# Giving each step's streamed weights their own start inside the ring buffers

## The chip, the cores and the metric

The kernel runs on one core of a Trainium2 chip. The metric is the device time of one execution in microseconds; the times given are medians of several runs. A profile shows one execution, with its own time.

## The reference

One layer of a hybrid model for a sequence of 256 tokens and a width of 1024, all in float32:

```python
h = _rmsnorm(x, norm_w) * (1 + scale) + shift          # shift, scale, gate = split(c @ w_ada + b_ada)
(qa, ka, va, za, qm, km, vm, zm, om, ig, fg, ga, gm) = jnp.split(h @ w_in, SPLIT_IDX, axis=-1)
qa, ka = _rmsnorm(heads(qa), q_norm_w), _rmsnorm(heads(ka), k_norm_w)
ya = (merge(_moba_attention(qa, ka, heads(va), rel_bias)) * jax.nn.silu(za)) @ w_att_proj
qm, km = jnp.split(jax.nn.silu(_causal_dwconv(jnp.concatenate([qm, km], -1), conv_w, conv_b)), 2, -1)
hm = jax.nn.sigmoid(om) * _mlstm_chunkwise(qm, km * ML_HEAD_DIM ** -0.5, vm, ig + b_igate, fg + b_fgate)
hm = _rmsnorm(hm, ml_norm_w)
ym = (merge(hm) * jax.nn.silu(zm)) @ w_ml_proj
y = jax.nn.sigmoid(ga) * ya + jax.nn.sigmoid(gm) * ym
return x + gate * (y @ w_out)
```

With 256 tokens the attention has one block, so it is plain causal attention with a bias. Most of the work is thirteen projections of 256 x 1024 by 1024 x 1024, whose weights are read once from DRAM.

## The kernel before

A first phase computes `h` and, row by row of `w_in`, the projections `qa` and most of `ka`. It leaves `h` transposed in SBUF as two parts, `hTh` and `hTl`: the value as it stands in the matmul format float32r, and the remainder. Every weight is split in the same way into `wh` (high) and `wl` (low), and each product is the sum of three matmuls: high by high, high by low, low by high.

The second phase, which the change touches, is a list of chunks, each half a projection (512 columns) and four steps long; a step covers two blocks of 128 rows of a weight. Three kinds differ in which operand TensorE holds and which it streams:

- `tok` (`ka`, `va`, `out`): a 128 x 128 block of the activations is held (stationary), and the weights are streamed (moving), up to 512 columns at once. Lines 1160 to 1162; the last chunk of `out` is written apart, lines 1184 to 1186, as one group of 512 columns and two groups of 256.
- `str` (`zm`, `vm`, `om`): a whole projection by Strassen's seven products in 14 steps of six matmuls. The weights, or sums of weight blocks, are streamed too (lines 1149 to 1151), against `hTh`, `hTl` or the sums `Sh`, `Sl` of their blocks.
- `ws` (`za`, `qm`, `km`, `att`, `ga`, `gm`, `ml`): the weights are held and the activations streamed, 256 columns at once (lines 1170, 1174, 1175). 24 matmuls a step.

`split(g)` prepares step `g`: ScalarE casts the loaded weights into `wh` (line 461, or 459 for `ml`), and VectorE, or GpSimd in ten steps, subtracts it from the weights into `wl` (line 467, or 465). It runs four steps ahead of the matmuls, in two rings of five buffers, `wh` and `wl`. A ring buffer holds `RING = 1152` floats a partition (4608 bytes), of which a step uses 1024, as two rows of 512. The order of all work is that of the code, per engine; hooks (`at`, `between`, `ahead`) place the attention, the gates and the mLSTM between the steps. In each ring buffer a `ws` step begins at float `WS_AT = 80`, and every other step at 0.

The two rings, `hTh` and `hTl` lie at fixed places: each ring buffer begins at a multiple of 512 bytes in its partition, `hTh` and `hTl` 256 bytes past one, and their blocks of 128 columns follow 512 bytes apart.

Of the kernel before, what the change touches and what calls it, by code (L numbers as in the profile page):

```python
# [10 lines left out]
F32R = mybir.dt.float32r  # L11
# [13 lines left out]
RING, WS_AT = 1152, 80  # L25
# [39 lines left out]
def tile_hybrid(ctx: ExitStack, tc: tile.TileContext, x, c, params, params2, rel_t, w_row, ada_mod, ada_gate,  # L65
# [89 lines left out]
    def modulate(k, parts="ij"):  # L155
        kc = slice(k, k + 1)
        if "i" in parts:
            nc.scalar.activation(hTh[:, k], xnT[:, k], AF.Identity, scale=Ab[:, kc], bias=Bb[:, kc])
        if "j" not in parts:
            return  # L160
        hf[k] = ph.tile([128, S], F32, name="hf", bufs=2)
        nc.scalar.activation(hf[k], xnT[:, k], AF.Identity, scale=Ab[:, kc], bias=Bb[:, kc])
# [96 lines left out]
    def some(*what):  # L259
        return lambda k: [mm_row(k, ch, (i,)) for ch, i in what]  # L260
# [19 lines left out]
    for step in P1_STEPS:  # L280
        op, k = step[0], int(step[1])
        if op == "L":
            next_loads(k)
        else:
# [5 lines left out]
                 a=modulation_scale, b=modulation_shift, i=lambda k: modulate(k, "i"), j=lambda k: modulate(k, "j"),  # L290
                 P=lambda k: mm_row(k, 0), Q=lambda k: mm_row(k, 1, (0, 1)), q=lambda k: mm_row(k, 1, (2,)),
                 N=lambda k: mm_row(k, 2), M=lambda k: mm_row(k, 3),
                 n=some((2, 0), (2, 1), (3, 0), (3, 1)), m=some((2, 2), (3, 2)),
# [31 lines left out]
    C, step0, owner = {}, [], []  # L325
# [86 lines left out]
    hl = ctx.enter_context(tc.tile_pool(name="hl", bufs=1, reuse_waits="tile"))  # L412
# [19 lines left out]
    HB = 5  # L432
    pool_lo = set()
    pool_lo.update((step0[C["ml", 0]] + 2, step0[C["ml", 0]] + 3))
    for nm, hf in (("qm", 0), ("qm", 1), ("km", 0), ("km", 1)):
        s = (start("km") if (nm, hf) == ("qm", 1) else done(nm, hf)) + 4
        pool_lo.update((s, s + 1))

    def split(g, between=()):
        ch = chunks[owner[g]]  # L440
        if ch["kind"] == "str":
            j = g - step0[owner[g]]
            w = form(ch["name"], j // 2)[:, 2 * (j % 2):2 * (j % 2) + 2]
        else:
            li, ks, cs = raw_of[g]
            w = rawt[li][:, ks, cs]
        n = ch["n"]
        at0 = WS_AT if ch["kind"] == "ws" else 0
        h = hl.tile([128, RING], F32R, name="wh", bufs=HB)[:, at0:at0 + 1024].rearrange("p (k n) -> p k n", k=2)[:, :, 0:n]
        l = hl.tile([128, RING], F32R, name="wl", bufs=HB)[:, at0:at0 + 1024].rearrange("p (k n) -> p k n", k=2)[:, :, 0:n]  # L450
        e = nc.gpsimd if g in pool_lo else nc.vector
        kp = 2 * (g - step0[owner[g]])
        cols = [(kk, prm2[:, P_ML + kp + kk:P_ML + kp + kk + 1]) for kk in range(2)] if ch["name"] == "ml" else []
        if cols and g in pool_lo:
            for kk, wcol in cols:
                nc.scalar.activation(w[:, kk], w[:, kk], AF.Copy, scale=wcol)
            cols = []
        for kk, wcol in cols:
            nc.scalar.activation(h[:, kk], w[:, kk], AF.Copy, scale=wcol)
        if not cols:  # L460
            nc.scalar.copy(h, w)  # L461
        for fn, a in between:
            fn(*a)
        for kk, wcol in cols:
            nc.vector.scalar_tensor_tensor(l[:, kk], w[:, kk], wcol, h[:, kk].bitcast(F32), op0=OP.mult, op1=OP.subtract)
        if not cols:
            e.tensor_tensor(l, w, h.bitcast(F32), op=OP.subtract)  # L467
        whl[g] = (h, l)
# [18 lines left out]
    def form(name, p):  # L487
        if p in (1, 6):
            return T["t1" if p == 1 else "t4", name]
        return block(name, *((0, 0), None, (0, 0), (1, 0), (0, 1), (1, 1))[p])  # L490
# [48 lines left out]
    def left(p, k):  # L539
        i = (None, 0, 1, None, 2, 3, None)[p]  # L540
        if i is not None:
            return T["Sh"][:, i, k], T["Sl"][:, i, k]
        k, t = {0: (k, 0), 3: (4 + k, 0), 6: (4 + k, 1)}[p]
        return hTh[:, k, t * 128:(t + 1) * 128], hTl[:, k, t * 128:(t + 1) * 128]
# [433 lines left out]
    def ev_out(pt, c0, n, t):  # L978
# [7 lines left out]
              zm=ev_zm, vm=ev_vm, om=ev_om, ga=ev_ga, gm=ev_gm, ml=ev_ml)  # L986
# [111 lines left out]
    for g in range(A):  # L1098
        split(g)
        for fn, a in early.get(g, []):  # L1100
            fn(*a)
        consumed.update(cons.get(g, []))
    pump()
    for g in range(NG):
        ci = owner[g]
        kp = g - step0[ci]
        ch = chunks[ci]
# [5 lines left out]
        if g + A < NG:  # L1113
            split(g + A, hooks_between.get(g, []))
            consumed.update(cons.get(g + A, []))
# [24 lines left out]
        wh, wl = whl[g]  # L1140
        if ci == NCH - 1:
            continue
        if ch["kind"] == "str":
            p = kp // 2
            o = mmt[ci][(0, 2, 0, 1, 0, 2, 0)[p]]
            for kk in range(2):
                k = 2 * (kp % 2) + kk
                a, b = left(p, k)
# [4 lines left out]
        for kk in range(2):  # L1153
            k = 2 * kp + kk
            first, last = k == 0, k == KT - 1
            if ch["kind"] == "tok":
                for t in range(2):
                    a, b = sh_[:, k, t * 128:(t + 1) * 128], sl_[:, k, t * 128:(t + 1) * 128]
# [19 lines left out]
    for t, c0, n in ((0, 0, 512), (1, 0, 256), (1, 256, 256)):  # L1178
        pt = ps.tile([128, n], F32, name="mm", bufs=2)
        for k in range(KT):  # L1180
            wh, wl = whl[step0[ci] + k // 2]
            wh, wl = wh[:, k % 2, c0:c0 + n], wl[:, k % 2, c0:c0 + n]
            a, b = T["yh"][:, k, t * 128:(t + 1) * 128], T["yl"][:, k, t * 128:(t + 1) * 128]
# [51 lines left out]
```

## Time and profile before

| | |
|---|---|
| median of 3 runs | 348.6 us (348.18 to 348.78) |
| the profiled execution | 348.25 us, span 346.5 us |
| TensorE matmuls | 340.8 us busy (98% of the span), 2314 |
| TensorE weight loads | 311.9 us, beside the matmuls |
| VectorE | 293.1 us (85%) |
| ScalarE | 240.4 us (69%) |
| GpSimd | 87.8 us (25%) |
| DMA | 83.72 MB, mean 242 GB/s |

In the rows PE is TensorE, PEld its weight loads, ACT ScalarE, DVE VectorE, POOL GpSimd. A row of the timeline gives the start in us, the duration in us, the engine, the line, the operation, output and inputs, and the shape; a matmul's inputs are the tile that it streams, or the other, in the program's order of names, and `128x512` is the streamed columns. A row of a group ends with the count, the busy time in us and the mean duration in ns. A row of waits gives who waited for whom, the sum in us, the number of times, and the longest. Durations of matmuls have modelled ends: they overlap the next matmul, and the distance between two starts tells the rate.

On TensorE the stages follow one another so: the first phase to 52 us; `ka` 52.1 to 57.9; `va` 58.0 to 87, with attention scores between its steps; `za` and `qm` to 141.6; `zm` to 160.9; `km` and `att` to 209.8; `vm` to 228.9; `ga` to 250.8; `om` to 269.8; `gm` to 298.4, with the last of the mLSTM between its steps; `ml` to 320.2; `out` to the end.

### The profile page before, as it was taken

To read this page: it belongs to the slowest core of one execution; us is meant where nothing else is said; L and a number is where in the kernel's file an instruction comes from. 1 tells how busy PE (TensorE), PEld (TensorE's weight loads), DVE (VectorE), ACT (ScalarE), POOL (GpSimd) and SP (SyncE) were. 2 spreads that over 40 slices of the span, in tenths; PEclk is the share of its full clock that TensorE was granted. 3 is DMA by queue.
4 is the path that set the end of the run, shared out by engine and by line. 5 is a ranking of instruction groups with operands and counts; after the bars stand their busy time and mean duration, and the time that the engine had idled before them with its cause. 6 is when DMAs were issued, how large, how long until landed. Compare 5 with 4: busy or idle time off the path is not lost.

```text
span 346.5 us, 6040 instructions
## 1 busy us (share of the span) xinstructions
PE 340.8 (98%) x2314; PEld 311.9 (90%) x2314; DVE 293.1 (85%) x423; ACT 240.4 (69%) x372; POOL 87.8 (25%) x90
## 2 busy tenths in 40 slices
PE   8999999999999999999999999999999999999995
PEld 5887889888999999888999998899988999999885
DVE  4899994897988887999796899998988988988852
ACT  3776787989977756699688657875497768745500
POOL 4950003765200715002353273001000023400000
PEclk9999999999999999999999999999999999999999
DMA  8999999996468399188750973929969379073011
GB/s 297 417 420 422 417 387 341 235 246 274 137 231 305 58 338 296 38 304 363 268 220 2 357 195 67 387 90 350 280 188 419 113 272 384 3 270 155 0 62 61
DMA packets 29534, 83.72 MB, mean 242 GB/s; under 512 B 2109, under 2 KB 5185, under 8 KB 28994
## 3 DMA queue, kind: packets, MB, share of 16 engines
q1 hardware_dynamic: 26944, 78.08, 61.5%
q0 software_dynamic: 2112, 4.19, 7.0%
q10 hardware_dynamic: 450, 1.07, 1.0%
q8 instruction: 18, 0.29, 0.3%
q14 instruction: 10, 0.08, 0.1%
HBM read 81.89 MB, written 1.45 MB: 241 GB/s over the span
## 4 chain that ended last, share of the span: by engine, by line
PE 82%; DMA 8%; POOL 4%; DVE 2%; ACT 2%; issue 1%; SPq 0%; DVEq 0%; POOLq 0%; ACTq 0%
PE mm L1170 15%; PE mm L1174 15%; PE mm L1175 15%; DMA raw<-in_w_row_dram 8%; PE aux L1149 6%; PE aux L1150 6%; PE aux L1151 5%; PE pm L186 4%; POOL ms L608 2%; PE mm L1162 2%; PE mm L1161 2%; PE mm L1160 2%; PE mm L1186 1%; PE mm L1185 1%; PE mm L1184 1%
## 5 line engine op out<-in xcount | busy, mean ns | idle before, releaser
L467 DVE TENSOR_TENSOR wl<-raw,wh 128x1024 fp32r<-128x1024 f32 (+1 forms) x90 | 109.0, 1237 | 18.9 <-ACT wh L461 18.8
L461 ACT CAST wh<-raw 128x1024 fp32r<-128x1024 f32 (+1 forms) x100 | 101.4, 1031 | 25.9 <-PE mm L1174 18.2
L1170 PE MATMUL mm<-hTh,wh 128*128 128x256 f32 x320 | 89.7, 280 | 0.0
L1174 PE MATMUL mm<-hTl,wh 128*128 128x256 f32 x320 | 88.8, 277 | 0.0
L1175 PE MATMUL mm<-hTh,wl 128*128 128x256 f32 x320 | 88.6, 277 | 0.0
L1175 PEld LDWEIGHTS mm<-hTh,wl 128*128 128x128 f32 x320 | 60.3, 188 | 0.0
L1170 PEld LDWEIGHTS mm<-hTh,wh 128*128 128x128 f32 x320 | 60.1, 188 | 0.1
L1174 PEld LDWEIGHTS mm<-hTl,wh 128*128 128x128 f32 x320 | 60.1, 188 | 0.0
L467 POOL TENSOR_TENSOR wl<-raw,wh 128x1024 fp32r<-128x1024 f32 x10 | 24.4, 2458 | 52.0 <-ACT wh L461 52.0
L1160 PE MATMUL mm<-wh,hTh 128*128 128x512 f32 (+1 forms) x64 | 23.9, 373 | 0.0
L1161 PE MATMUL mm<-wl,hTh 128*128 128x512 f32 (+1 forms) x64 | 23.2, 363 | 0.0
L1162 PE MATMUL mm<-wh,hTl 128*128 128x512 f32 (+1 forms) x64 | 23.2, 363 | 0.0
L175 DVE TENSOR_TENSOR wrl<-raw,wrh 128x512 fp32r<-128x512 f32 (+1 forms) x24 | 18.1, 776 | 1.0 <-ACT wrh L170 0.7
L1149 PE MATMUL aux<-wh,Sh 128*128 128x512 f32 x48 | 18.7, 389 | 0.0
L1150 PE MATMUL aux<-wl,Sh 128*128 128x512 f32 x48 | 18.7, 389 | 0.0
L1151 PE MATMUL aux<-wh,Sl 128*128 128x512 f32 x48 | 18.7, 389 | 0.0
L170 ACT CAST wrh<-raw 128x512 fp32r<-128x512 f32 (+1 forms) x24 | 15.7, 684 | 3.6 <-DMA raw<-in_w_row_dram 3.6
L1170 PE MATMUL mm<-yah,wh 128*128 128x256 f32 x64 | 17.8, 279 | 0.0
L1174 PE MATMUL mm<-yal,wh 128*128 128x256 f32 x64 | 17.7, 276 | 0.0
L1175 PE MATMUL mm<-yah,wl 128*128 128x256 f32 x64 | 17.7, 276 | 0.0
L1175 PE MATMUL mm<-ymh,wl 128*128 128x256 f32 x64 | 17.7, 276 | 0.0
L1170 PE MATMUL mm<-ymh,wh 128*128 128x256 f32 x64 | 17.7, 276 | 0.0
(251 smaller groups left out, 830.4 us busy)
## 6 DMA issues: line engine op xcount, KB each, us to landing
raw<-in_w_in_dram SPq DMA_DIRECT2D x36, 1024.0 KB, 7.3
adat<-in_ada_mod_dram SPq DMA_DIRECT2D x16, 512.0 KB, 9.4
gw<-in_ada_gate_dram SPq DMA_DIRECT2D x4, 1024.0 KB, 9.8
raw<-in_w_att_proj_dram SPq DMA_DIRECT2D x4, 1024.0 KB, 9.8
raw<-in_w_ml_proj_dram SPq DMA_DIRECT2D x4, 1024.0 KB, 5.0
raw<-in_w_out_dram SPq DMA_DIRECT2D x4, 1024.0 KB, 5.5
raw<-in_w_row_dram SPq DMA_DIRECT2D x4, 896.0 KB, 12.4
raw<-in_w_in_dram POOLq DMA_DIRECT2D x3, 1024.0 KB, 12.7
```

Source lines behind the costliest of these rows:

```text
L175: e.tensor_tensor(l[:, cs], wrow[k][:, cs], h[:, cs].bitcast(F32), op=OP.subtract)
L461: nc.scalar.copy(h, w)
L467: e.tensor_tensor(l, w, h.bitcast(F32), op=OP.subtract)
L1149: nc.tensor.matmul(o, a, wh[:, kk], start=k == 0 and p in (0, 1, 3), stop=False, skip_group_check=True)
L1150: nc.tensor.matmul(o, a, wl[:, kk], start=False, stop=False, skip_group_check=True)
L1151: nc.tensor.matmul(o, b, wh[:, kk], start=False, stop=k == 3, skip_group_check=True)
L1160: nc.tensor.matmul(o, a, wh[:, kk], start=first, stop=False)
L1161: nc.tensor.matmul(o, a, wl[:, kk], start=False, stop=False)
L1162: nc.tensor.matmul(o, b, wh[:, kk], start=False, stop=last)
L1170: nc.tensor.matmul(o, wh[:, kk, cs], sh_[:, k], start=first and i % 2 == 0, stop=False, skip_group_check=True)
L1174: nc.tensor.matmul(o, wh[:, kk, cs], sl_[:, k], start=False, stop=False, skip_group_check=True)
L1175: nc.tensor.matmul(o, wl[:, kk, cs], sh_[:, k], start=False, stop=last and i % 2 == 1, skip_group_check=True)
```

## The change

The start inside the ring buffers becomes a function of the chunk and of the step `j` in it. `ws` steps keep float 80. In floats of 4 bytes, for `wh` and `wl` alike: `ka` 16 j; `va` 8 (4 half + j); `zm` 4 j; `vm` 64 + 4 j; `out` 16 (4 half + j). For `om`, `wh` stays at 0 and `wl` begins at 8 j. In bytes that is 0 to 192 for `ka`, 0 to 224 for `va`, 0 to 208 for `zm`, 256 to 464 for `vm`, 0 to 416 for `om`'s low part, 0 to 448 for `out`. The buffers, their number and their places stay as they are, and so do all instructions, their order on each engine and their waits.

```diff
+    def at_of(ch, j):
+        if ch["kind"] == "ws":
+            return WS_AT, WS_AT
+        a = {"ka": 16 * j, "va": 8 * (4 * ch["half"] + j), "zm": 4 * j, "vm": 64 + 4 * j, "om": 0, "out": 16 * (4 * ch["half"] + j)}[ch["name"]]
+        return a, 8 * j if ch["name"] == "om" else a
+
     def split(g, between=()):
...
         n = ch["n"]
-        at0 = WS_AT if ch["kind"] == "ws" else 0
-        h = hl.tile([128, RING], F32R, name="wh", bufs=HB)[:, at0:at0 + 1024].rearrange("p (k n) -> p k n", k=2)[:, :, 0:n]
-        l = hl.tile([128, RING], F32R, name="wl", bufs=HB)[:, at0:at0 + 1024].rearrange("p (k n) -> p k n", k=2)[:, :, 0:n]
+        a0, a1 = at_of(ch, g - step0[owner[g]])
+        h = hl.tile([128, RING], F32R, name="wh", bufs=HB)[:, a0:a0 + 1024].rearrange("p (k n) -> p k n", k=2)[:, :, 0:n]
+        l = hl.tile([128, RING], F32R, name="wl", bufs=HB)[:, a1:a1 + 1024].rearrange("p (k n) -> p k n", k=2)[:, :, 0:n]
```

## The prediction

> **What bounds the kernel now.** I read the busy table first, then the chain that ended last, the waits of TensorE's weight loads, and then the starts of single matmuls in the timeline, because the change touches nothing but addresses. The profiled execution took 348.25 us, 0.35 us under the median of the three runs (348.6 us); its span is 346.5 us. From the page:
>
> ```profile
> PE 340.8 (98%) x2314; PEld 311.9 (90%) x2314; DVE 293.1 (85%) x423; ACT 240.4 (69%) x372; POOL 87.8 (25%) x90
> PEclk9999999999999999999999999999999999999999
> PE 82%; DMA 8%; POOL 4%; DVE 2%; ACT 2%; issue 1%; SPq 0%; DVEq 0%; POOLq 0%; ACTq 0%
> ```
>
> TensorE is the bound, at a full granted clock throughout. A shorter matmul therefore shortens the kernel, except where another engine ends the wait last. There are two such places near the change. The chain leaves TensorE from 58 to 83 us, and the waits of the weight loads show where it comes back:
>
> ```profile
> 58.08 1.07 ACT wh L461
> 59.17 1.00 DVE wl L467
> ...
> 82.57 0.33 DVE P L735
> 82.91 0.20 DVE P L737
> 83.18 0.33 PE aux L756
> ```
>
> ```profile
> PEld aux L1149 <- ACT wh L461: 0.4, 1, 0.4
> PEld aux L756 <- DVE st L737: 0.3, 1, 0.3
> ACT wh L461 <- PE mm L1162: 0.8, 1, 0.8
> ```
>
> So through the `va` steps TensorE runs beside a chain of ScalarE, VectorE and GpSimd work and arrives 0.3 us early. What is gained in `va` is waited away at 83.18 us, and a loss of up to 0.3 us there is free. The chain's first piece, the cast of 58.08, waited for a matmul of the line that multiplies `ka`, so a gain in `ka` does pass on.
>
> Now the single matmuls. The column "mean ns" holds a modelled end, so I use the distance between starts. The timeline of TensorE, at the ends of runs of equal matmuls:
>
> ```profile
> 142.96 0.39 PE L1149 MATMUL aux<-wh,hTh 128*128 128x512 f32 x1
> 156.56 0.39 PE L1149 MATMUL aux<-wh,Sh 128*128 128x512 f32 x1
> 298.40 0.28 PE L1170 MATMUL mm<-ymh,wh 128*128 128x256 f32 x1
> 320.16 0.40 PE L1160 MATMUL mm<-wh,hTh 128*128 128x512 f32 x1
> 231.71 0.28 PE L1170 MATMUL mm<-hTh,wh 128*128 128x256 f32 x1
> 250.75 0.40 PE L1149 MATMUL aux<-wh,hTh 128*128 128x512 f32 x1
> 282.59 0.28 PE L1170 MATMUL mm<-hTh,wh 128*128 128x256 f32 x1
> 288.24 0.27 PE L939 MATMUL aux<-ident,omt 128*128 128x128 f32 x1
> 52.09 0.29 PE L1160 MATMUL mm<-wh,hTh 128*128 128x264 f32 x1
> 57.86 0.38 PE L650 MATMUL aux<-ident,gt 128*36 128x128 f32 x2
> 336.53 0.28 PE L1184 MATMUL mm<-wh,hTh 128*128 128x256 f32 x1
> 342.16 0.28 PE L1186 MATMUL mm<-wh,hTl 128*128 128x256 f32 x1
> ```
>
> The pairs are to be read as rates. Ten Strassen steps of six 512-column matmuls: 13.60 us / 60 = 226.7 ns each. The eight steps of `ml`, 24 matmuls of 256 columns each with the ring as stationary operand: 21.76 / 192 = 113.3 ns, half of it, so both run at one rate per column (0.443 ns). Seven steps of `ga`: 19.04 / 168 = 113.3 ns. But two steps of `gm`, the same shape: 5.65 / 48 = 117.7 ns. The 48 of 264 columns in `ka`: 5.77 / 48 = 120.2 ns, where the common rate gives 116.9. And the last 256-column ones: 5.63 / 47 = 119.8 ns. The same work on the same idle-free TensorE thus costs 113 to 120 ns, and what differs is where its operands lie and how it was entered. The built program's addresses say where: in `ka`, in the Strassen steps whose stationary operand is `hTh` or `hTl`, and in `out`, the moving start minus the start of the weights loaded meanwhile is 256 modulo 512 bytes. In `ml` it is 192 (the 80-float offset), in `ga` and `gm` 448. A difference that is 0 modulo 128 goes with 120 ns; 64 modulo 128 goes with 113 or 118.
>
> **The change part by part.** Every engine keeps its instructions, their order and their waits; no tile moves and no buffer grows. Only the start inside a ring buffer changes: of the cast that writes `wh`, the subtraction that reads it and writes `wl`, and the matmuls that stream them. No transfer touches these tiles.
>
> (1) *`ka`, 48 matmuls.* Step 0 keeps its start; steps 1 to 3 move by 64, 128 and 192 bytes, to differences of 320, 384 and 448. The best row leaves 116.9 ns: 36 x 3.3 = 0.12 us at most, nothing at least. I take the pattern modulo 128, so steps 1 and 3 gain: 24 x 3.3 = -0.08 us, and it passes on through the cast of 58.08.
>
> (2) *`out`, last chunk, the 48 narrow matmuls.* The four steps move by 256, 320, 384 and 448 bytes, to differences of 0, 64, 128 and 192. All four at 113.3: 48 x 6.5 = -0.31 us; none: 0. By the same pattern two of the four gain, 24 x 6.5 = -0.16 us. What follows them is only the last sum and store, so all of it counts. The chunk's 512-column matmuls, and the first half of `out`, run at 227 ns and stay.
>
> (3) *The 512-column matmuls of `va`, `zm`, `vm`, `om`.* They run at the common rate already, since the load is over long before the stream ends. What they can lose or gain is in the entry. When the 256-column mode ends, the first six take longer:
>
> ```profile
> 141.57 0.40 PE L1149 MATMUL aux<-wh,hTh 128*128 128x512 f32 x1
> 141.81 0.40 PE L1150 MATMUL aux<-wl,hTh 128*128 128x512 f32 x1
> 142.04 0.39 PE L1151 MATMUL aux<-wh,hTl 128*128 128x512 f32 x1
> ```
>
> From 141.57 to 142.96 are six in 1.39 us, against 1.36 at the rate: 0.03 us. The first steps of `zm`, `om` and `out` begin at 0 as before, so their entries stay; only `vm` starts elsewhere, by 256 bytes (0 to -0.03 us; I take 0, as 256 is 0 modulo 128). `va` has such entries behind each group of attention matmuls, but there 0.3 us are covered by the wait at 83.18; gain 0.
>
> (4) *Starts that are no multiple of 64 bytes*, as `zm`, `vm` and half of `va` and `om`'s low part now have. No ring operand has one today. The nearest rows are the `vaug` matmuls, 258 columns whose head starts lie at multiples of 8 bytes (head size 1032 bytes), against `vml` of 256 columns at multiples of 1024, both between 269 and 283 us:
>
> ```profile
> L901 PE MATMUL aux<-vaug,SD 128*128 128x258 f32 x10 | 2.8, 281 | 0.0
> L899 PE MATMUL aux<-vaug,SD 128*128 128x258 f32 x9 | 2.5, 283 | 0.0
> L900 PE MATMUL aux<-vml,SD 128*128 128x256 f32 x9 | 2.5, 280 | 0.0
> ```
>
> Two more columns explain 0.9 ns, so a stray start costs 0.1 to 2.1 ns in 258 columns, 0.2 to 4.2 ns in 512. Affected are 48 matmuls of `va`, some 60 each of `zm` and `vm`, 14 of `om`, 182 in all: 0.04 to 0.76 us. Both lines stream the same `vaug` tiles, most of them from stray starts; L901 shows that such a start need not cost, so I take the low end: +0.04 us. The Trainium skill, "SBUF — State Buffer", section Specifications, gives cachelines of 16 bytes with a penalty for each crossing; every new start is a multiple of 16 bytes, so by it a row crosses as many lines as before and this term is zero. No run here separates 0 from 0.04 us.
>
> (5) *Casts and subtractions.* ScalarE's cast has a mean of 1051 ns around the `zm` steps and 1049 ns around `ga` and `gm`, so the 320-byte start of the latter costs nothing:
>
> ```profile
> L461 ACT CAST wh<-raw 128x1024 fp32r<-128x1024 f32 x9 | 9.2, 1051 | 0.6 <-PE aux L1151 0.4
> L461 ACT CAST wh<-raw 128x1024 fp32r<-128x1024 f32 x5 | 5.2, 1049 | 5.7 <-PE mm L1174 5.7
> ```
>
> I take 0 on both engines; TensorE covers them, and where that cover is gone (58 to 83 us, and the 0.4 us wait at 158 us) 2 ns in each of some ten casts are 0.02 us.
>
> Sum: -0.08 - 0.16 + 0.04 = -0.20 us, from 348.25 to 348.05 in a profiled execution; against the median, 348.4 us.
>
> **The rivals.** A change under 0.2% (0.7 us) cannot be told from none: the three runs alone lie 0.6 us apart.
>
> *Nothing at all changes.* If weight load and moving stream never met, the 113 and 120 ns would come from something else, such as the stationary operand's side, and the start would be free: 348.6 us. For it speaks that the 512-column matmuls hold 226.7 ns at any ring place; against it that one shape runs at three rates. The Trainium skill, "SBUF — State Buffer", section Who interferes with whom, gives TensorE two independent read ports and says that it never waits on anyone; by it this rival is right. The rates above do not agree with that rule, but no run here yet moves the start alone.
>
> *Faster by more than I take: the slow mode of `gm` goes too.* `gm` runs at 117.7 ns for six steps while `ga` at the same difference of 448 runs at 113.3, so the mode is one of how the chunk is entered, and `om` stands right ahead of it. Leaving it gives 6 x 24 x 4.4 = -0.63 us; with all of (1) and (2) and the `vm` entry, -0.12 - 0.31 - 0.03, it is -1.09 us: 347.5 us. Against it: between `om` and `gm` nine `vaug` and `vml` matmuls stand, which the change leaves alone, and the mode survived two more such groups. It decides once `gm` leaves the mode in its first step.
>
> *Slower: every step's new place starts the drift anew.* Now all steps of a chunk share one difference, and the 0.03 us of entry is paid once. If each of the moved steps (7 of `va`, 13 of `zm`, 14 of `vm`, 13 of `om`, 7 of `out`: 54) pays it, that is 1.6 us less the 0.3 us covered in `va` and less the 0.2 us of the forecast's gains: 349.7 us. Against it: ring buffers 512 bytes apart pass without any such cost, and a step of 16 bytes is small beside the 64 that divide good from bad. From about 40 paying steps on it is slower by over 0.7 us.
>
> **How the numbers follow.** The forecast's case (some part of -0.6 to +0.2 us) 0.42, nothing at all 0.13, the faster rival and whatever else gains over 0.7 us 0.28, the slower one, with the 4.2 ns end of (4) in it, 0.17. So faster 0.28, same 0.55, slower 0.17. The forecast's own range is 348.0 to 348.8 us. To leave out no more than 2 in 10 the range must take in most of the faster rival (347.5, with the spread of runs 347.2) and the half-paid slower one (349.4).
>
> **What would show it.** In the changed profile the last 48 matmuls take about 5.5 us in place of 5.75, `ka` 5.69 in place of 5.77; `zm` to `om` keep 226.7 ns with starts moved; the six `gm` steps keep 117.7 ns; the wait at 83.18 stays within 0.2 us of 0.3. A step of `zm` over 1.37 us would show the drift or the stray starts; `gm` at 113.3 the faster rival; unmoved 120 ns in `ka` and `out` the first. I am wrong if the rate per column of the 512-column matmuls itself depends on the start, which no row shows since all lie at multiples of 64 bytes.

## The result and the profile after

The changed kernel is slower: 352.87 us against 348.39 us before. The medians differ by 4.5 us; the ratio of the runs is 1.0119 (95% interval 1.0100 to 1.0137), about 4.2 us. A second measurement, beside the last experiments, gave 352.36 against 348.36 us (1.0116, 1.0096 to 1.0136). The profiled execution took 353.44 us with a span of 351.6 us, 5.2 us over the span before.

From the page of the changed kernel:

```profile
PE 346.1 (98%) x2314; PEld 316.9 (90%) x2314; DVE 292.8 (83%) x423; ACT 240.1 (68%) x372; POOL 83.7 (24%) x90
PEclk9999999999999999999999999999999999999999
PE 98%; DVE 0%; POOL 0%; issue 0%; POOLq 0%
```

TensorE is busy 5.3 us longer with the same 2314 matmuls at the same full clock; VectorE and ScalarE are as busy as before. The chain is now TensorE for 98%: the detour through VectorE and GpSimd at 58 to 83 us is gone, since TensorE no longer arrives early. So the loss is in the matmuls themselves. Their timeline, at the ends of runs of equal matmuls, as for the kernel before (line numbers are 6 higher from line 439 on; in the experiments they shift with each edit):

```profile
51.98 0.29 PE L1166 MATMUL mm<-wh,hTh 128*128 128x264 f32 x1
57.84 0.38 PE L656 MATMUL aux<-ident,gt 128*36 128x128 f32 x2
144.38 0.39 PE L1155 MATMUL aux<-wh,hTh 128*128 128x512 f32 x1
161.11 0.39 PE L1155 MATMUL aux<-wh,hTh 128*128 128x512 f32 x1
165.45 0.28 PE L1176 MATMUL mm<-hTh,wh 128*128 128x256 f32 x1
185.24 0.28 PE L1176 MATMUL mm<-yah,wh 128*128 128x256 f32 x1
341.82 0.28 PE L1190 MATMUL mm<-wh,hTh 128*128 128x256 f32 x1
347.33 0.28 PE L1192 MATMUL mm<-wh,hTl 128*128 128x256 f32 x1
```

`ka`: 5.86 / 48 = 122.1 ns (120.2 before). Twelve steps of `zm`: 16.73 / 72 = 232.4 ns (226.7 in the undisturbed steps before). Seven steps of `km`: 19.79 / 168 = 117.8 ns. The narrow matmuls at the end: 5.51 / 47 = 117.2 ns (119.8). `km` is the surprise, for none of its addresses changed. Its groups, before and after, over seven steps; the last number ahead of the second bar is the mean in ns, whose modelled end adds 163 ns to the distance between starts:

```profile
L1170 PE MATMUL mm<-hTh,wh 128*128 128x256 f32 x56 | 15.5, 276 | 0.0
```

```profile
L1176 PE MATMUL mm<-hTh,wh 128*128 128x256 f32 x58 | 16.3, 281 | 0.0
```

Below, 276 stands for 113.3 ns and 281 for 117.8 ns; a held-weight (`ws`) chunk is called fast at the one and slow at the other. The time of each chunk, from the start of its first matmul to that of the next chunk's first (for `out`, to the end), shows the whole loss. The columns behind "before" are differences to it, in us, one profiled execution each; from early_only on they are the experiments below:

| chunk | before | after | after, again | early_only | late_only | last_back | last_only | last_zm | last_64 | const | pad64 | after_extra1 | no_extra |
|---|---|---|---|---|---|---|---|---|---|---|---|---|---|
| ka | 5.90 | +0.10 | +0.10 | +0.10 | 0 | +0.10 | 0 | 0 | 0 | 0 | 0 | +0.10 | 0 |
| va | 29.20 | -0.13 | +0.02 | -0.09 | -0.01 | -0.15 | +0.06 | 0 | -0.12 | +0.03 | +0.02 | -0.11 | +0.01 |
| za | 29.72 | **+0.76** | +0.02 | +0.02 | 0 | 0 | +0.02 | 0 | 0 | 0 | +0.31 | +0.02 | +0.65 |
| qm | 24.66 | **+0.80** | 0 | 0 | 0 | 0 | 0 | 0 | 0 | 0 | +0.21 | 0 | -0.04 |
| zm | 19.33 | +0.20 | +0.20 | +0.01 | +0.20 | +0.18 | +0.03 | +0.05 | +0.04 | +0.01 | +0.03 | +0.20 | 0 |
| km | 21.88 | **+0.84** | +0.84 | 0 | +0.84 | +0.84 | 0 | +0.84 | +0.02 | +0.01 | 0 | +0.01 | +0.73 |
| att | 27.03 | **+0.83** | +0.83 | 0 | +0.83 | +0.83 | 0 | +0.83 | 0 | 0 | 0 | 0 | +0.83 |
| vm | 19.07 | +0.46 | +0.46 | 0 | +0.46 | +0.44 | +0.05 | 0 | +0.03 | 0 | 0 | +0.46 | 0 |
| ga | 21.88 | **+0.84** | +0.84 | 0 | +0.84 | +0.84 | +0.84 | 0 | -0.01 | 0 | 0 | +0.01 | +0.73 |
| om | 20.14 | +0.40 | +0.40 | 0 | +0.40 | +0.39 | 0 | 0 | +0.16 | +0.45 | 0 | +0.41 | 0 |
| gm | 27.51 | +0.01 | +0.01 | 0 | +0.01 | 0 | 0 | 0 | 0 | 0 | 0 | +0.01 | +0.08 |
| ml | 21.76 | 0 | 0 | 0 | 0 | 0 | 0 | 0 | 0 | 0 | 0 | 0 | +0.85 |
| out | 26.31 | +0.17 | +0.17 | 0 | +0.19 | +0.18 | 0 | 0 | +0.27 | +0.29 | -0.01 | +0.18 | +0.01 |

In the first profile 4.07 us lie in five chunks that hold the weights and were not touched (`za`, `qm`, `km`, `att`, `ga`), and 1.2 us in the chunks that stream them. In the second profile `za` and `qm` are fast, and 2.5 us and 1.35 us remain: that is the common part, and it adds up to 3.9 us.

### The profile page after: what moved, and what is told of

It is laid out like the page before. It is cut to its first block, busy times and chain, and to the rows that moved or that the text cites. A ratio compares the mean times of both kernels' runs of the same rounds, so it can differ in the third digit from the quotient of the medians.

```text
span 351.6 us, 6040 instructions
## 1 busy us (share of the span) xinstructions
PE 346.1 (98%) x2314; PEld 316.9 (90%) x2314; DVE 292.8 (83%) x423; ACT 240.1 (68%) x372; POOL 83.7 (24%) x90
## 4 chain that ended last, share of the span: by engine, by line
PE 98%; DVE 0%; POOL 0%; issue 0%; POOLq 0%
PE mm L1176 15%; PE mm L1180 15%; PE mm L1181 15%; PE pm L186 9%; PE aux L1156 6%; PE aux L1155 6%; PE aux L1157 6%; PE mm L1166 4%; PE mm L1168 4%; PE mm L1167 4%; PE pg L186 2%; PE xps L244 1%; PE mm L1192 1%; PE pc L220 1%; PE mm L1190 1%; PE mm L1191 1%
## 5 line engine op out<-in xcount | busy, mean ns | idle before, releaser
L1176 PE MATMUL mm<-hTh,wh 128*128 128x256 f32 x320 | 90.9, 284 | 0.0
L1180 PE MATMUL mm<-hTl,wh 128*128 128x256 f32 x320 | 90.0, 281 | 0.0
L1181 PE MATMUL mm<-hTh,wl 128*128 128x256 f32 x320 | 89.9, 281 | 0.0
L467 ACT CAST wh<-t 128x1024 fp32r<-128x1024 f32 x12 | 12.6, 1050 | 8.7 <-PE mm L1180 5.5
```

The lines of the kernel that those rows point to most:

```text
L1176: nc.tensor.matmul(o, wh[:, kk, cs], sh_[:, k], start=first and i % 2 == 0, stop=False, skip_group_check=True)
L1180: nc.tensor.matmul(o, wh[:, kk, cs], sl_[:, k], start=False, stop=False, skip_group_check=True)
L1181: nc.tensor.matmul(o, wl[:, kk, cs], sh_[:, k], start=False, stop=last and i % 2 == 1, skip_group_check=True)
```

## The experiments

Two questions: what the new starts do to the streamed matmuls, and how they reach chunks that they do not touch. I began with the theory "entry" (a held-weight chunk takes its rate from the step ahead of it) against "state" (TensorE carries a slow state from one chunk to the next until something resets it).

**early_only and late_only.** The new starts in two chunks alone, or in all but these:

```diff
+        if ch["name"] not in ("ka", "va"):     # late_only: in ("ka", "va")
+            return 0, 0
```

> Only ka and va have the new starts; zm, vm, om and out begin at 0 as before. The changed kernel loses 4.07 us in five held-weight chunks (za, qm, km, att, ga at 117.7 ns a matmul in place of 113.3) and 1.2 us in the streamed ones. Theory 'entry': a held-weight chunk's rate is set by the step just ahead of it, so za and qm are slow (+1.56 us) and km, att, ga fast again: about 349.9 us. Rival 'state': a moved start puts TensorE into a slow state that it carries until something resets it, so all five stay slow: about 352.4 us.

> Only zm, vm, om and out have the new starts; ka and va begin at 0. Both theories have za and qm fast. Entry: km, att and ga slow, +2.5 us, and the streamed chunks +1.2 us: about 352.1 us. State: the same, if zm's moved starts set it. A third possibility, that only ka or va matter: 349.6 us.

Measured: 348.39 us (1.0007, 0.9993 to 1.0022) and 352.11 us (1.0105, 1.0090 to 1.0120). The groups of `km`, early_only first:

```profile
L1178 PE MATMUL mm<-hTh,wh 128*128 128x256 f32 x57 | 15.8, 276 | 0.0
```

```profile
L1178 PE MATMUL mm<-hTh,wh 128*128 128x256 f32 x57 | 16.0, 281 | 0.0
```

All of the loss that repeats comes with the new starts of `zm`, `vm`, `om` and `out`; `ka` and `va` are free, as in `va` the slower matmuls eat up the early arrival at 83 us. Both theories missed that `za` and `qm` stay fast in early_only.

**last_back and last_only.** The last step of each chunk at its old place, or only that of `va` and `vm` at its new one:

```diff
# last_back
+        if j == (13 if ch["kind"] == "str" else 3) and (ch["name"], ch["half"]) in (("va", 1), ("zm", 0), ("vm", 0), ("om", 0)):
+            return 0, 0
# last_only
+        if (ch["name"], ch["half"], j) not in (("va", 1, 3), ("vm", 0, 13)):
+            return 0, 0
```

> As the changed kernel, but the last step of va, zm, vm and om begins at 0 again. Entry: za, qm, km, att and ga are fast, 4.07 us come back: about 348.8 us. State: the slow state was set steps earlier and is carried over one step at 0: about 352.8 us.

> As the kernel before, but the last step of va (224 bytes) and the last of vm (464 bytes) have the new starts. Entry: za, qm and ga slow, km and att fast: +2.4 us, about 350.8 us. State: all five slow from za on: about 352.5 us. If a single step does nothing: 348.4 us.

Measured: 352.48 us (1.0114, 1.0096 to 1.0131) and 349.52 us (1.0035, 1.0021 to 1.0048). In last_back `km`, in last_only first `km` and then `ga`:

```profile
L1178 PE MATMUL mm<-hTh,wh 128*128 128x256 f32 x58 | 16.3, 281 | 0.0
```

```profile
L1178 PE MATMUL mm<-hTh,wh 128*128 128x256 f32 x51 | 14.1, 276 | 0.0
...
L1178 PE MATMUL mm<-hTh,wh 128*128 128x256 f32 x52 | 14.6, 281 | 0.0
```

One moved step of six matmuls (`vm`'s last, at 464 bytes) is enough to slow all eight steps of `ga`; but one step at the old place does not undo the steps ahead of it. So neither theory holds in its plain form. The reading that fits both runs is that the streamed steps hand TensorE over in some phase, that the phase decides the rate of the next chunk, and that a step does not wipe out the phase that it was given. No row shows a phase; the word stands for whatever is handed over. `va`'s last step did nothing to `za`, with attention work between them.

**last_zm and last_64.** Other starts in the last step of `zm` and `vm`: 208 and 256 bytes, then 64 and 128 (last_64 also sets all of `om` to 64 and the first half of `out` to 128):

```diff
# last_zm, in floats
+        a = {("zm", 13): 52, ("vm", 13): 64}.get((ch["name"], j), 0)
# last_64
+        a = {("zm", 13): 16, ("vm", 13): 32}.get((ch["name"], j), 0)
+        if ch["name"] in ("om", "out") and ch["half"] == 0:
+            a = 16 if ch["name"] == "om" else 32
```

> The kernel before with only the last step of zm at 208 bytes (its start in the change) and only the last of vm at 256 bytes. Entry phase: one step is enough to spoil the small matmul at km's head, and 256 bytes is harmless: km and att slow, +1.67 us, ga fast: 350.1 us. If a single step of zm is not enough, or the 0.4 us wait in zm decides instead: 348.4 us. If any change of start between two steps spoils it: ga slow too, 350.9 us.

> The kernel before with the last step of zm at 64 bytes, the last of vm at 128, all of om at 64 and the first half of out at 128. Entry phase, with the steady rates of the run with constant starts (64 bytes 228.9 ns, 128 bytes 232.5): km and att fast, ga slow (+0.84), om +0.19, first half of out +0.27: about 349.7 us. If the chunk and not its start sets the rate, om stays at 232 (+0.45) and out's half at 233.

Measured: 350.04 us (1.0055, 1.0035 to 1.0074) and 349.05 us (1.0022, 1.0012 to 1.0031). In last_zm `km` and then `ga`, in last_64 `km` and then `ga`:

```profile
L1176 PE MATMUL mm<-hTh,wh 128*128 128x256 f32 x56 | 15.7, 281 | 0.0
...
L1176 PE MATMUL mm<-hTh,wh 128*128 128x256 f32 x54 | 14.9, 276 | 0.0
```

```profile
L1178 PE MATMUL mm<-hTh,wh 128*128 128x256 f32 x50 | 13.8, 276 | 0.0
...
L1178 PE MATMUL mm<-hTh,wh 128*128 128x256 f32 x50 | 13.8, 276 | 0.0
```

A last step at 208 bytes (of `zm`) or 464 (of `vm`) slows the next chunk; at 64 (of `zm`), 128 or 256 (of `vm`) it does not. I had expected 128 to slow `ga`.

**const.** One start for all steps of a chunk, in place of one for each:

```diff
+        a = {"zm": 16, "vm": 64, "om": 32, "out": 8 if ch["half"] == 0 else 128}.get(ch["name"], 0)
+        return a, a
```

> Each streamed chunk has one start for all its steps: zm 64 bytes, vm 256, om 128, first half of out 32, second half 512; ka and va 0. 'Difference': the rate of a streamed matmul depends on its start against the weights being loaded (mod 256), not on a change between steps. Then vm and the second half of out keep 226.7 ns and ga stays fast, while zm, om and the first half of out run at 231 to 235 all along (zm +0.4 us, om +0.4, out +0.2), and km and att are slow (+1.67 us): about 351.1 us. 'Drift at each change': a chunk with one start pays 0.03 us once, and km, att, ga stay fast: 348.5 us.

Measured: 349.12 us (1.0026, 1.0005 to 1.0046). Groups of `vm` (256 bytes), `om` (128) and the first half of `out` (32):

```profile
L1157 PE MATMUL aux<-wh,Sl 128*128 128x512 f32 x16 | 6.2, 389 | 0.0
```

```profile
L1157 PE MATMUL aux<-wh,Sl 128*128 128x512 f32 x16 | 6.3, 394 | 0.0
```

```profile
L1168 PE MATMUL mm<-wh,hTl 128*128 128x512 f32 x14 | 5.5, 395 | 0.0
```

So a start alone, the same in all steps, slows the streamed matmuls. 389 is 226.7 ns; at 128 and 32 bytes every step, not the first alone, takes 4 to 7 ns more a matmul (the starts of whole steps give 232.5 and 233.3 ns on average), and at 64 bytes 2.2 ns (steps of `zm` of 1.373 us / 6 = 228.9 ns). `om` at 64 bytes in last_64 lost 0.16 us, which fits. A change from step to step is not needed. Nor is it the place to which the casts and subtractions write meanwhile: beside the last four steps of `om` they fill `gm`'s buffers from 320 bytes, not 128, and the steps whose matmuls run through stay at 232.5 to 233.0 ns. That `zm` shows only +0.01 us is cover: before, it held a 0.4 us wait for a cast at 157.7 us, and the slower matmuls arrive later at it. My expectation for `km` and `att` failed: they stayed fast, as after `zm` at 64 bytes in last_64.

The start is not the whole rule, though. The fifth step of `zm` begins at 64 bytes in the changed kernel too, with the same operands held. Its first matmul and the next step's, in the changed kernel and then in const:

```profile
148.56 0.40 PE L1155 MATMUL aux<-wh,Sh 128*128 128x512 f32 x1
149.96 0.39 PE L1155 MATMUL aux<-wh,Sh 128*128 128x512 f32 x1
```

```profile
147.84 0.39 PE L1155 MATMUL aux<-wh,Sh 128*128 128x512 f32 x1
149.22 0.39 PE L1155 MATMUL aux<-wh,Sh 128*128 128x512 f32 x1
```

1.40 us against 1.37, that is 233.0 ns a matmul behind steps at 16, 32 and 48 bytes and 228.9 behind steps at 64. At 64 bytes the streamed matmuls have two rates as well, and no run shows what chooses between them. At 256 bytes none of this is seen: the ninth step of `om` in the changed kernel, whose low part begins there, takes 226.7 ns between steps that take 231 to 232.

**pad64.** Is it the place of the streamed operand, or its distance from the weights loaded meanwhile? 64 unused bytes ahead of `hTh` shift it, the rings and all later tiles together:

```diff
+    consts.tile([128, 16], F32, name="pad64")
     hTh = consts.tile([128, KT, S], F32R, name="hTh")
```

> The kernel before, with 64 unused bytes ahead of hTh, so that hTh, hTl, the rings and all later tiles lie 64 bytes further on, and every difference between streamed and loaded operands stays. If the difference decides: the time of before, 348.4 us, every chunk within 0.05 us. If the place of the streamed start by itself (mod 256 or 128) decides: streamed chunks at 231 to 235 ns and slow held-weight chunks, about 352 us.

Measured: 349.64 us (1.0031, 1.0019 to 1.0044). A group of `vm`:

```profile
L1150 PE MATMUL aux<-wh,hTh 128*128 128x512 f32 x7 | 2.7, 389 | 0.0
```

The streamed chunks, now 64 bytes on everywhere, and `km`, `att`, `ga` keep their time to 0.03 us. In const 64 bytes of the start alone cost 2.2 ns a matmul, so the place itself does not matter here, but the distance to something that was shifted along. I take this to be the weights loaded meanwhile; no run moved them alone. The 1.1 us by which the median is higher are half explained: 0.52 us lie in `za` and `qm`, the rest ahead of the second phase (its start is 0.9 us later in this profile, but 52.0 to 53.0 us over all kernels). The Trainium skill, "SBUF — State Buffer", section Who interferes with whom, says that TensorE's two read ports are independent and that it never waits on anyone. If the loaded weights are what the distance counts from, const and pad64 together do not agree with that.

**after_extra1 and no_extra.** Six 8-column matmuls stand ahead of or inside held-weight chunks (the table `EXTRA`; 0 is ahead of a block's first matmul, 1 behind it). In after_extra1 the changed kernel has those of `km` and `ga` one matmul later; in no_extra the kernel before has none:

```diff
-    EXTRA = {..., ('km', 0, 0, 0): 0, ('ga', 0, 0, 0): 0, ('gm', 1, 2, 0): 1}
+    EXTRA = {..., ('km', 0, 0, 0): 1, ('ga', 0, 0, 0): 1, ('gm', 1, 2, 0): 1}     # after_extra1
+    EXTRA = {}                                                                   # no_extra
```

> The changed kernel, with the small matmul of km and of ga put between the first and the second matmul of the chunk, as gm has it, in place of ahead of the first. If that place resets the slow state: km, att and ga are fast again, -2.5 us, about 350.1 us. If the state comes from the starts and a small matmul does not reset it: 352.5 us.

> The kernel before without the six 8-column matmuls that stand at the head of or inside held-weight chunks. If the slow state is carried until one of them resets it: gm's last 1.7 steps and all of ml stay slow, +0.2 and +0.86 us, and za to ga as in before: about 349.4 us. If each chunk's entry sets its state: za, qm, km, ga may turn slow (0.8 us each, up to +3.2 us) and ml stays fast. If the small matmuls do nothing: 348.2 us.

Measured: 349.96 us (1.0040, 1.0023 to 1.0058) and 352.34 us (1.0106, 1.0089 to 1.0123). `km` in after_extra1; then `km` and `ml` in no_extra:

```profile
L1176 PE MATMUL mm<-hTh,wh 128*128 128x256 f32 x51 | 14.1, 276 | 0.0
```

```profile
L1170 PE MATMUL mm<-hTh,wh 128*128 128x256 f32 x49 | 13.8, 281 | 0.0
...
L1174 PE MATMUL mm<-yml,wh 128*128 128x256 f32 x49 | 13.8, 281 | 0.0
```

These are the two decisive runs. The kernel before runs `km`, `att`, `ga` and `ml` at 113.3 ns because small matmuls stand where they stand: without them all four are slow, `ml` behind a `gm` that stays slow to its end, `att` behind `km`. Neither the carried state alone (349.4 us) nor the entry alone (`ml` fast) gives that; both act. In the changed kernel the same small matmuls at the head of `km` and `ga` do not help; moved by one matmul they do, and 2.5 us come back. What is left over the kernel before, 1.4 us in the medians, is mostly the streamed chunks (1.24 us in this profile). The small matmuls are not the only way back: in no_extra `za` is slow as well, but `qm` behind it turns fast in its third step (117.8 to 113.3 ns), behind attention work and without one.

**gm_kick.** Can the same be had in `gm`, which is slow in both kernels?

```diff
+    EXTRA = {..., ('gm', 0, 1, 0): 1, ('gm', 0, 3, 0): 1, ('gm', 1, 2, 0): 1}
```

> The kernel before with two more 8-column matmuls in gm, between the first and second matmul of its second and fourth step. If that place resets the slow state as it did in km and ga: four steps go from 117.7 to 113.3 ns, -0.43 us, less 0.12 us for each of the two: -0.19 us, 348.3 us, no difference in time but visible in gm (27.32 in place of 27.51 us). If it does not reset: +0.24 us (27.75 us).

Measured: 353.01 us (1.0133, 1.0118 to 1.0148). `gm` took 31.40 us in place of 27.51, and `ml` 22.62 in place of 21.76. The wait, the timeline, and TensorE by windows (span and busy time in us, number, granted clock, DMA share, GB/s):

```profile
PE aux L1173 <- ACT den L904: 2.0, 1, 2.0
```

```profile
278.01 0.27 PE L1173 MATMUL aux<-hTh,wh 128*128 128x8 f32 x1 [1.97 <-ACT den L904]
...
278.80 0.41 PE L1175 MATMUL mm<-hTh,wl 128*128 128x256 f32 x1
279.01 0.41 PE L1170 MATMUL mm<-hTh,wh 128*128 128x256 f32 x1
```

```profile
270.80:275.70 4.90, 4.90 (x44) 1.00 0.12 25
278.30:281.80 3.50, 3.50 (x19) 0.53 0.86 300
```

The first small matmul takes one of four PSUM buffers that the mLSTM was still reading, so TensorE stood still for 2 us, and then ran at a granted clock of 0.53: 213 ns a matmul for 3 us. Once the clock was back the matmuls behind the first kick took 113.3 ns, and so did those behind the second, up to the end of the next step; so the place does reset the rate there. But from the transposes behind that step on, `gm` was slow again, the old small matmul in it did not help this time, and `ml` stayed slow: moving one shifts what the later ones meet. No version came out that beats the kernel before.

**after_again.** The changed kernel once more:

> The changed kernel once more. In its profile za and qm were slow (+1.56 us), in three other kernels with the same starts in ka and va (but for the last step of va in one) they were fast. If za and qm fall either way from execution to execution: this profile may have them fast and a span of 350.0 to 350.3 us; if the change fixes them slow: 351.6 us again.

Measured: 352.36 us, profile span 350.7 us (with a first phase longer by 0.5 us), `za` and `qm` fast. The attention's matmuls between the last two steps of `va`, first in the profile with slow `za`, then in the one with fast:

```profile
82.80 0.38 PE L738 MATMUL aux<-kT,qT 128*128 128x128 f32 x2
83.02 0.27 PE L762 MATMUL aux<-ident,P 128*128 128x128 f32 x1
```

```profile
83.28 0.39 PE L738 MATMUL aux<-kT,qT 128*128 128x128 f32 x2
83.59 0.33 PE L762 MATMUL aux<-ident,P 128*128 128x128 f32 x1
```

0.22 us in the one, 0.31 us in the other: where TensorE waited for the attention there, even by 0.1 us, `za` came out fast. So those 1.56 us fall either way from execution to execution. In early_only and after_extra1, which have the same starts in `ka` and `va` and a fast `za`, the wait is shorter still, 0.03 to 0.04 us, one matmul later. That the short wait itself sets the rate was not tried; it rests on these four profiles.

## Why the prediction was wrong

I forecast 348.4 us, at most 349.4, with 0.55 for no difference; the kernel took 352.9 us. By its steps:

- *That TensorE bounds, and that `va` is covered by the wait at 83 us*: right. `va`'s eight steps ran slower, and the chunk took -0.13 to +0.02 us.
- *(1) `ka`*: wrong in sign. 120.2 ns became 122.1: +0.10 us in place of -0.08, and the two steps that were to gain 3.3 ns a matmul (64 and 192 bytes) lost 0.9 and 3.4. The pattern "64 modulo 128 is good" came from rows with the weights held, and did not carry over to streamed ones.
- *(2) the narrow matmuls of `out`*: the number was near by luck, -0.12 us against -0.16. Two steps were to go from 120 to 113.3 ns and two to stay; in fact all four moved, to 117.7, 118.1, 117.7 and 115.5. (The sign set for them, 5.5 us for the 48, did not follow from -0.16 either, which gives 5.6; it was 5.6.) And the wide matmuls of the same steps gave the gain back (the second half of `out` -0.01 us).
- *(3) "They run at the common rate already, since the load is over long before the stream ends"*: the step that failed. The rate was common because all differences were 256 modulo 512 (0 serves as well), not because the load was hidden. The other differences tried cost 2 to 7 ns a matmul on average; over the 512-column matmuls of the changed kernel the mean distance between starts rose from 227.5 to 232.1 ns. I priced the term at 0; in the second profile the streamed chunks lost 1.35 us, net of what `va` and the wait in `zm` cover. The last sentence of the prediction named just this, a rate that depends on the start, as the way to be wrong, but gave it no price; and its reason, that all starts were multiples of 64 bytes, was too mild, as 64 and 128 bytes cost too.
- *(4) the stray starts*: the bound of 4.2 ns was too low (6.6 ns at 32 bytes) and put on the wrong thing: 128 and 64 bytes, no stray starts, cost 5.8 and 2.2 ns.
- *(5) casts and subtractions*: right; both engines are as busy as before.
- *The rivals.* I had seen that `gm`'s slow rate is a matter of how the chunk is entered, and used it for one rival only, in which `gm` gets faster. The same row said that every other held-weight chunk could be entered badly: six slow steps in `gm` at 0.11 us each make 0.84 us for an eight-step chunk, 4.2 us for five, on the table from the start. That is the term missing from the sum and from the range, and it makes up 2.5 us of the loss, in one profile 4.07. The slower rival had the right sign, 349.7 us, for another mechanism, a drift paid anew at each change of start; const showed that no change between steps is needed, though the fifth step of `zm` took more behind steps of other starts (233.0 against 228.9 ns).

What stays open: why starts at 32 or 128 bytes cost more than at 64, why 64 has two rates, and what the small matmul must meet to help. The runs give rates for 32, 64, 128 and 256 bytes and outcomes for a last step at 64, 128, 208, 256 and 464, and no rule for them.

## What to carry to other kernels

Where one operand streams while the next weights load, treat the place of one against the other as a tuned quantity even if no wait shows it: read the distance between starts of equal matmuls, and treat two rates for one shape as a warning that an address or an entry can switch them. A changed rate in one stage can cost more in untouched stages behind it than in its own, so price each later stage at its slowest observed rate before calling a change harmless. And a small matmul that looks idle may be what keeps the next 20 us fast; take such tuning anew after anything ahead of it moves.

## What the runs showed of the hardware

In chunks of one start, a streamed float32r matmul of 512 columns takes 226.7 ns at a distance of 0 or 256 bytes (modulo 512) between its start and the next weights, and with the start moved on from there 228.9 at 64 bytes, 232.5 at 128 and 233.3 at 32; behind steps of other starts the 64 bytes took 233.0. With the weights held, one of 256 columns runs at 113.3 or 117.8 ns for 20 us on end, at the same addresses, by how it was entered. And in gm_kick a wait of 2.0 us was followed by a granted clock of 0.53 for 3 us. The Trainium skill, "TensorE: Matmul & The Clock Gate", section Part 1: The HAM clock gate, gives at least one idle window of about 3.4 us for that; in this one profile 2.0 us came before it.
